# Attention times V over four query tiles at once instead of two, in a two-layer encoder

## The chip, the core and the metric

The kernel runs on one core of a Trainium2 chip, in one launch. The metric is the device time in microseconds, the median over several runs. The engines are called by the names that the profile uses: PE (matrix multiplication, with PEld for its weight loads), DVE (vector), ACT (scalar functions and copies), POOL (a second, slower vector engine) and SP, which here only issues transfers.

## The reference, cut to what matters

Two layers work on 1024 tokens of width 1024, one sequence, float32. Each normalizes, projects, runs a bidirectional attention with 8 heads, gates the result with SiLU(z), projects out and adds to the residual.

```python
# layer 0, differential attention, per block of 128 queries
sc = einsum('bqhcd,bkhcd->bhcqk', qb, k) * scale      # two score maps per head, c = 0, 1
p = softmax(sc, axis=-1)
p = p[:, :, 0] - lam * p[:, :, 1]
o = einsum('bhqk,bkhd->bqhd', p, v)                   # v: 1024 keys x 128 per head
# then RMSNorm of each head's 128 values, gate, output projection

# layer 1, latent attention (MLA)
sc = (einsum('bqhd,bkhd->bhqk', qn, k_nope) + einsum('bqhr,bkr->bhqk', qp, k_pe)) * scale
o = einsum('bhqk,bkhd->bqhd', softmax(sc, axis=-1), v)
```

The part in question is the last product of each layer, P times V ("PV" below).

## The kernel before, in words

**Precision.** A float32 product is made of three matmuls of a fast format: each operand is split in a high part and a low rest, and high x high, high x low and low x high are summed in PSUM (`mm3`). So everything that goes into a matmul exists twice (`pth` and `ptl` for P transposed, the two halves of `vt` for V).

**Tiles of an attention.** A head has 1024 queries: eight tiles of 128, in two halves of four. For each tile, scores against all 1024 keys are built in PSUM (eight matmuls of 512 columns in layer 0, where there are two score maps; ten in layer 1), DVE takes the negative row maximum (L393), ACT the exponential with its row sum (L395). In layer 0 DVE then combines both maps into `e` (L775), and the next tile's first maximum is queued behind that; the second map's PSUM buffer is held until then. PE turns `e` around by transposes, four blocks of 128 x 128 into one PSUM bank (L376, bank `tr`, a single buffer), ACT copies the bank into `pth` (L378) and DVE subtracts that into `ptl` (L379). A tile takes two such turns, `kh` = 0 for the first 512 keys and 1 for the rest.

**PV before.** V is the weight (a 128 x 128 block for each key tile, high or low), P^T the moving operand, and the result o^T stands in one PSUM bank per half (`pv`, 512 columns). Two query tiles share a set of four P^T buffers, each of four key tiles x 256 columns (4 KB per partition), out of six. So PV runs for every second tile, with 256 columns: 8 key tiles x 3 matmuls for a pair, in two parts of 12 (`kh` = 0 and 1). When both pairs of a half are done, `close` normalizes and gates the half.

**The order of work.** It is written out by hand in `after_scores` and `run_tails`. With tile i's scores, the tile before (`last`) gets its first turn behind the scores, the one before that (`prev`) its second turn amid the scores, and PV of `prev`, if it is the second of a pair, follows. Between these points stand numbers of filler steps from the tables `FILL0`, `FILL1` (six or four per tile, eight tiles per head) and `FILL7` (layer 0's last head): a step is three matmuls of 512 columns of the projection that feeds the next head (queries, keys, gate z), with the transfers of its weights, their splitting on ACT and POOL, and the copies of its result. In each layer's last head, steps of the output projection (`Pre.step`, six matmuls) are run from the seventh tile on. Behind the loop `run_tails` finishes the last two tiles. A scheduler with its own cost model then orders the instructions of each engine by the program's order and its estimate of when each is ready, so that an engine's order in the trace is not always that of the program.

**V.** Layer 1 has its values for heads 4 to 7 computed and stored to DRAM shortly before its attention starts (`v1_tile`, `store_v`), through temporary tiles that live in the P^T buffers' pool (tag "pt"). `load_v` brings a head's V back, two transfers of 512 KB, into three buffers.

The functions that the change touches:

## Time and profile before

| | before |
|---|---|
| device time, median of 3 runs | 1458.1 us (1456.93 to 1460.11) |
| profiled execution, span from first to last instruction (its only time) | 1457.5 us |
| PE busy | 1396.9 us, 96% |
| PE weight loads busy | 1166.4 us, 80% |
| DVE, ACT, POOL busy | 63%, 50%, 43% |
| matmuls | 7388, of which 1536 are PV |

Layer 0's attention with its filler lies at about 178 to 705 us of the span, layer 1's at about 1010 to 1368. In a row of instructions in order of time there stand the start in us, the duration in us, engine, line, operation, what it writes and reads, shape and count (x4: four merged in one row); in brackets the idle time of the engine just before and what ended it. In a row of groups there stand the count, the busy time in us, the mean duration of one in ns and the idle time before. A row of stretches gives for each engine the busy us and the number of instructions, then the granted clock of PE, the share of the transfer engines in use and GB/s. Matmuls overlap in the pipeline: the duration of one is longer than the distance to the next.

### The profile page before, as it was taken

The numbers are of one execution on the slowest core, as the hardware profiler recorded it, in microseconds if no ns is written. First come the engines' busy times: TensorE is split into PE (matmuls) and PEld (weight loads), VectorE is DVE, ScalarE is ACT, GpSimd is POOL, SyncE is SP. The second block draws the span as 40 slices with busy tenths as digits, with TensorE's granted clock in tenths as the row PEclk, the third lists the DMA queues.
The fourth block names the chain that finished last, engine by engine and source line by source line (L and its number), as shares of the span: only waits on it lengthen the run. The fifth ranks groups of instructions, "written<-read, shape, count | busy, mean of one in ns | idle before, by whom it ended". The sixth has DMA issues, their size and how long they took to land. (4 is left out here: it accounts for less than half of the span.)

```text
span 1457.5 us, 20649 instructions
## 1 busy us (share of the span) xinstructions
PE 1396.9 (96%) x7388; PEld 1166.4 (80%) x7388; DVE 917.9 (63%) x1362; ACT 727.8 (50%) x1287; POOL 627.6 (43%) x493
## 2 busy tenths in 40 slices
PE   5999999999999999998999879989999999999997
PEld 4778788888888887886787768867888888888886
DVE  6656777767777767687355964544666555555355
ACT  5622365656566665565343433334455554545342
POOL 4416164656465555543641455422141331412572
PEclk9999999999999999999999989999999999999999
DMA  9787723333332424237743145398443432336563
GB/s 329 228 252 237 245 67 99 85 99 87 102 93 82 114 68 117 59 87 261 253 144 123 44 152 173 107 289 211 146 125 123 118 104 65 110 97 215 181 234 141
DMA packets 135527, 213.70 MB, mean 147 GB/s; under 512 B 19072, under 2 KB 56064, under 8 KB 135424
## 3 DMA queue, kind: packets, MB, share of 16 engines
q1 hardware_dynamic: 135424, 212.38, 47.7%
q8 instruction: 58, 0.95, 0.3%
q14 instruction: 45, 0.37, 0.1%
HBM read 137.92 MB, written 50.80 MB: 129 GB/s over the span
## 5 line engine op out<-in xcount | busy, mean ns | idle before, releaser
L378 ACT CAST pth<-tr 128x512 fp32r<-128x512 f32 x256 | 150.3, 587 | 281.7 <-PE tr L376 280.0
L393 DVE TENSOR_REDUCE nm<-s 128x1 f32<-128x1024 f32 x192 | 234.0, 1219 | 76.8 <-PE s L767 65.7
L379 DVE TENSOR_TENSOR ptl<-tr,pth 128x512 fp32r<-128x512 f32 x256 | 176.1, 688 | 140.1 <-ACT pth L378 139.6
L224 POOL TENSOR_TENSOR wl<-wraw,wh 128x512 fp32r<-128x512 f32 (+2 forms) x81 | 106.8, 1321 | 210.7 <-ACT wh L223 202.2
L395 ACT ACTIVATE e<-s,nm 128x1024 f32<-128x1024 f32 x128 | 143.7, 1122 | 31.8 <-DVE nm L393 26.2
L376 PE MATMUL tr<-ident,e 128*128 128x128 f32 x1024 | 154.6, 273 | 2.2 <-DVE ptl L379 1.9
L376 PEld LDWEIGHTS tr<-ident,e 128*128 128x128 f32 x1024 | 121.5, 140 | 42.9 <-DVE ptl L379 19.4
L178 PE MATMUL acc<-h0h,wh 128*128 128x512 f32 x360 | 150.8, 419 | 3.6 <-DVE v_hl L356 3.1
L178 PE MATMUL pv<-pth,vt 128*128 128x256 f32 x512 | 147.2, 287 | 0.0
L179 PE MATMUL pv<-ptl,vt 128*128 128x256 f32 x512 | 145.6, 284 | 0.0
L180 PE MATMUL pv<-pth,vt 128*128 128x256 f32 x512 | 144.6, 282 | 0.0
L180 PE MATMUL acc<-h0h,wl 128*128 128x512 f32 x360 | 142.8, 397 | 0.3 <-POOL wl L224 0.3
L179 PE MATMUL acc<-h0l,wh 128*128 128x512 f32 x360 | 142.1, 395 | 0.0
L1007 POOL TENSOR_TENSOR wol<-wor,woh 128x512 fp32r<-128x512 f32 x64 | 85.6, 1360 | 83.3 <-ACT woh L1006 78.9
L179 PEld LDWEIGHTS pv<-ptl,vt 128*128 128x128 f32 x512 | 97.7, 191 | 2.6
L178 PEld LDWEIGHTS pv<-pth,vt 128*128 128x128 f32 x512 | 97.6, 191 | 2.8 <-ACT pth L378 0.2
L180 PEld LDWEIGHTS pv<-pth,vt 128*128 128x128 f32 x512 | 97.7, 191 | 0.1
L320 POOL TENSOR_TENSOR rp_r<-rp_raw,cosT 128x512 f32<-128x512 f32 x38 | 49.8, 1311 | 94.9 <-ACT rp_raw L315 51.7
L325 POOL TENSOR_TENSOR rp_sw<-rp_sw,sinT 128x512 f32<-128x512 f32 x42 | 55.7, 1326 | 77.8 <-DMA rp_sw<-rp_raw 73.0
L767 PE MATMUL s<-ks,qa 128*128 128x512 f32 x256 | 82.0, 402 | 3.0 <-DVE e L775 2.7
L775 DVE SCALAR_TENSOR_TENSOR e<-s,z,e 128x1024 f32<-128x1024 f32 x64 | 82.1, 1283 | 2.1
L767 PE MATMUL s<-ks,qb 128*128 128x512 f32 x256 | 80.9, 395 | 0.0
(590 smaller groups left out, 3365.2 us busy)
## 6 DMA issues: line engine op xcount, KB each, us to landing
ada<-in_ada_ss SPq DMA_DIRECT2D x32, 512.0 KB, 5.8
wraw<-in_w_s SPq DMA_DIRECT2D x64, 256.0 KB, 2.9
vS<-v_hl SPq DMA_DIRECT2D x32, 512.0 KB, 5.3
vt<-vS SPq DMA_DIRECT2D x32, 512.0 KB, 3.9
wor<-in_w_out SPq DMA_DIRECT2D x64, 256.0 KB, 4.0
rp_sw<-rp_raw SPq DMA_DIRECT2D x168, 64.0 KB, 2.0
bc_s<-bc_d SPq DMA_DIRECT2D x34, 256.0 KB, 4.4
oS<-bc_s SPq DMA_DIRECT2D x30, 256.0 KB, 3.0
```

What stands on the lines that cost most here:

```text
L178: PE.matmul(psum, ah, bh, start=first, stop=False)
L179: PE.matmul(psum, ah, bl, start=False, stop=False)
L180: PE.matmul(psum, al, bh, start=False, stop=last)
L224: sub = (V if pair_of else G).tensor_sub(l_[:, :n], raw[:, :n], f32v(h_[:, :n]))
L376: PE.transpose(tr[:, j, :], p[:, kt * P : (kt + 1) * P], ident)
L378: mk["S"] = S.copy(pth[kh][:, :, dst], tr).ins
L379: mk["V"] = V.tensor_sub(ptl[kh][:, :, dst], tr, f32v(pth[kh][:, :, dst])).ins
L393: mk["V"] = V.reduce_max(nm, s_ps, axis=AX.X, negate=True).ins
L395: mk["S"] = S.activation(e, s_ps, AF.Exp, bias=nm, scale=1.0, accum_out=zs).ins
L767: PE.matmul(s_ps[:, kc * HF : (kc + 1) * HF], src[:, c, ql], KS[h][kc][:, c, :], start=fst, stop=not fst)
L775: combined.append(V.scalar_tensor_tensor(out=e0, in0=e1, scalar=z1[:, 0:1], in1=e0, op0=ALU.mult, op1=ALU.add).ins)
L1007: in_turn(G.tensor_sub(lo, raw, f32v(hi)))
```

## The change

PV runs once for four query tiles, with 512 moving columns: 8 key tiles x 3 matmuls for a half. P^T has four buffers of four key tiles x 512 columns (8 KB per partition), which are one half's high and low parts for both `kh`; each `kh` pair is allocated at the first tile's turn. The first part of PV (`kh` = 0) stands behind the fourth tile's first turn and two filler points later, the second part in the tile after. Within a part the order is no longer three matmuls per key tile, but all four key tiles of high x high, then low V x high P, then high V x low P. The filler tables are rewritten with the same sums per head. The V1 temporaries are halves of the larger P^T tiles (`vbuf`). The scratch for transfer descriptors is set to 1024 bytes.

```diff
@@ -38,8 +38,9 @@
 DEF = 7
 ROT = 3
 DEF1 = 0
-FILL0 = ((1, 2, 1, 1, 1, 0), (1, 1, 1, 1, 1, 1)) * 3 + ((1, 2, 1, 1, 1, 0), (1, 1, 1, 1, 1, 0))
-FILL1 = ((1, 0, 1, 0), (0, 1, 0, 0)) * 4
+FILL0 = ((1, 1, 1, 1, 1, 0), (1, 1, 1, 1, 1, 0), (1, 2, 1, 2, 1, 0), (1, 2, 1, 1, 1, 1)) + (
+    (1, 1, 1, 1, 1, 0), (1, 1, 1, 1, 1, 0), (1, 2, 1, 2, 1, 0), (1, 2, 1, 1, 1, 0))
+FILL1 = ((0, 1, 1, 0), (0, 0, 0, 0), (1, 1, 0, 0), (1, 0, 1, 0)) * 2
 SPL1 = 2
 Z_PRE = 16
 V_LATE = 6
@@ -55,7 +56,7 @@
 OP1 = (12, 4)
 LAST = [(((0, 1, 2, 3), 0, HF),), (((0, 1), 0, HF), ((2,), 0, HF), ((3,), 0, 256), ((3,), 256, HF))]
 Z_LAST = 4
-FILL7 = ((0, 1, 1, 1, 1, 0),) * 4
+FILL7 = ((0, 0, 0, 1, 1, 0), (0, 0, 0, 1, 0, 0), (0, 0, 0, 1, 0, 0), (0, 0, 0, 1, 0, 0), (0, 0, 0, 1, 1, 0))
 G_WAIT = 3
 G1_AT = 7
 VB = (2, 3)
@@ -351,7 +352,7 @@
             SP.dma_start(f32v(t[0:64, 1, :]), f32v(t[64:128, 1, :]))
 
     def store_v(l, sp, acc, tt, fh, tag="vst", bufs=None):
-        v = sp.tile([P, 2, HF], F32R, name="v_hl", tag=tag, bufs=bufs or VB[l])
+        v = sp() if callable(sp) else sp.tile([P, 2, HF], F32R, name="v_hl", tag=tag, bufs=bufs or VB[l])
         S.copy(v[:, 0, :], acc)
         V.tensor_sub(v[:, 1, :], acc, f32v(v[:, 0, :]))
         th, tl = tt // 4, tt % 4
@@ -379,13 +380,12 @@
         mk["V"] = V.tensor_sub(ptl[kh][:, :, dst], tr, f32v(pth[kh][:, :, dst])).ins
 
     def pv(o_, vt, pth, ptl, kh):
-        for j in range(4):
-            mm3(o_, vt[kh][:, 0, j, :], vt[kh][:, 1, j, :], pth[kh][:, j, :], ptl[kh][:, j, :], kh + j == 0, kh * 4 + j == NT - 1)
+        for lhs, rhs in ((0, pth), (1, pth), (0, ptl)):
+            for j in range(4):
+                PE.matmul(o_, vt[kh][:, lhs, j, :], rhs[kh][:, j, :], start=kh == j == lhs == 0 and rhs is pth, stop=kh == 1 and j == 3 and rhs is ptl)
 
     def alloc_pt(ap_):
-        pth = [ap_.tile([P, 4, 2 * P], F32R, name="pth", tag="pt", bufs=6) for _ in range(2)]
-        ptl = [ap_.tile([P, 4, 2 * P], F32R, name="ptl", tag="pt", bufs=6) for _ in range(2)]
-        return pth, ptl
+        return [ap_.tile([P, 4, 4 * P], F32R, name=n, tag="pt", bufs=4) for n in ("pth", "ptl")]
 
     def softmax_part(ap_, s_ps, zs, bufs=3):
 
@@ -863,30 +863,30 @@
     class Tail:
 
 
-        def __init__(self, qp, t, e, zz, c):
-            self.qp, self.t, self.e, self.zz, self.c = qp, t, e, zz, c
-            self.mate = tails[1]
+        def __init__(self, half, t, e, zz, c):
+            self.half, self.t, self.e, self.zz, self.c = half, t, e, zz, c
 
         def turn(self, kh):
-            if kh == 0:
-                self.pt = alloc_pt(self.c["pool"]) if self.t == 0 else self.mate.pt
-                self.mate = None
-            transpose_p(self.e, *self.pt, self.t, kh)
+            c = self.c
+            if self.t == 0:
+                if kh == 0:
+                    c["pt", self.half] = [], []
+                for d_, t in zip(c["pt", self.half], alloc_pt(c["pool"])):
+                    d_.append(t)
+            transpose_p(self.e, *c["pt", self.half], self.t, kh)
 
         def pv(self, kh):
-            c, qp = self.c, self.qp
-            if self.t == 0:
+            c = self.c
+            if self.t < 3:
                 return
             if kh == 0:
-                if qp == 0:
+                if self.half == 0:
                     c["vt"] = load_v(c["pool"], c["l"], c["h"])
-                if qp % 2 == 0:
-                    c["o_"] = bank("pv", "pv")
-                    c["open"](qp // 2)
-            cs = slice((qp % 2) * 256, (qp % 2) * 256 + 256)
-            pv(c["o_"][:, cs], c["vt"], *self.pt, kh)
-            if kh == 1 and qp % 2 == 1:
-                c["close"](qp // 2, c["o_"], self.zz)
+                c["o_"] = bank("pv", "pv")
+                c["open"](self.half)
+            pv(c["o_"], c["vt"], *c["pt", self.half], kh)
+            if kh == 1:
+                c["close"](self.half, c["o_"], self.zz)
 
     tails, hooks = [None, None], []
 
@@ -896,12 +896,10 @@
         prev.turn(1)
         fill(0)
         last.turn(0)
-        prev.pv(0)
-        prev.pv(1)
         fill(1)
         last.turn(1)
+        last.pv(0)
         fill(2)
-        last.pv(0)
         last.pv(1)
         tails[:] = [None, None]
 
@@ -911,12 +909,12 @@
         if last:
             last.turn(0)
         fill(n)
-        if prev:
-            prev.pv(0)
-        fill(n + 1)
         new = hooks[:]
         if prev:
             prev.pv(1)
+        fill(n + 1)
+        if last:
+            last.pv(0)
         fill(n + 2)
         for f in new:
             hooks.remove(f)
@@ -959,7 +957,7 @@
                     fill(2)
                     after_scores(fill, 3)
                 side.tick()
-                tails[:] = [tails[1], Tail(qp, t, e0, zz, ctx_)]
+                tails[:] = [tails[1], Tail(half, (qp * 2 + t) % 4, e0, zz, ctx_)]
                 if extra:
                     extra(qp * 2 + t)
         if late:
@@ -1131,7 +1129,7 @@
         head_out(o_, o, sq)
         return lambda: subln(o, sq, zz, 1, NH - 1, OT[NH - 1][1])
 
-    tail0 = attn0(NH - 1, lambda i: FILL7[i] if i < Z_LAST else (0,) * 6, extra0, late0)
+    tail0 = attn0(NH - 1, lambda i: FILL7[i] if i <= Z_LAST else (0,) * 6, extra0, late0)
     mk.clear()
     load_ot(OT[NH - 1][0], [oS[0][NH - 1, 0, i] for i in range(2)])
     st2b.close()
@@ -1625,7 +1623,7 @@
                     e = scores1(h, half, ti, zz)
                     fill(0)
                     after_scores(fill, 1)
-                tails[:] = [tails[1], Tail(qp, t, e, zz, ctx_)]
+                tails[:] = [tails[1], Tail(half, ti, e, zz, ctx_)]
                 if extra:
                     extra(qp * 2 + t)
         if late:
@@ -1636,9 +1634,17 @@
 
     stream1.step(6)
     v1_left = list(range(NT))
+    vbufs = []
+
+    def vbuf():
+        if not vbufs:
+            t = ap.tile([P, 4, 4 * P], F32R, name="v_hl", tag="pt", bufs=4)
+            vbufs.extend([t[:, :2, :], t[:, 2:, :]])
+        return vbufs.pop(0)
+
     for n, steps in zip(V1_AT, (steps1[0] - 6, 0)):
         for tt in v1_left[:n]:
-            v1_tile(tt, 1, ap, "pt", 6)
+            v1_tile(tt, 1, vbuf)
         del v1_left[:n]
         stream1.step(steps)
     side.flush()
@@ -1646,7 +1652,7 @@
     zz0 = sm.tile([P, 4], F32, name="zz1")
     first1 += [zz0, scores1(0, 0, 0, zz0)]
     for tt in v1_left:
-        v1_tile(tt, 1, ap, "pt", 6)
+        v1_tile(tt, 1, vbuf)
     stv.close()
     ap2 = pool(st5, "attn1b")
     for h in range(NH - 1):
@@ -1805,7 +1811,7 @@
     import concourse.bacc as bacc
     from concourse.bass_utils import run_bass_kernel_spmd
 
-    nc = bacc.Bacc("TRN2", target_bir_lowering=False, num_devices=1)
+    nc = bacc.Bacc("TRN2", target_bir_lowering=False, num_devices=1, dynamic_dma_scratch_size=1024)
     A = layout(inputs)
     arrays, aps = {}, {}
     for name, a in A.items():
```

## The prediction

> **What bounds the kernel now.** I read the page's totals and slices first, then the busy time by stages, then TensorE's (PE's) own order of time, since a "busy" PE says nothing about its pace.
>
> ```profile
> span 1457.5 us, 20649 instructions
> PE 1396.9 (96%) x7388; PEld 1166.4 (80%) x7388; DVE 917.9 (63%) x1362; ACT 727.8 (50%) x1287; POOL 627.6 (43%) x493
> L178 PE MATMUL pv<-pth,vt 128*128 128x256 f32 x512 | 147.2, 287 | 0.0
> L179 PE MATMUL pv<-ptl,vt 128*128 128x256 f32 x512 | 145.6, 284 | 0.0
> L180 PE MATMUL pv<-pth,vt 128*128 128x256 f32 x512 | 144.6, 282 | 0.0
> ```
>
> ```profile
> core 0: us, PE busy (x) PEld busy (x) DVE busy (x) ACT busy (x) POOL busy (x), PEclk, DMA share, GB/s
> 178.00:560.00 382.00, 381.69 (x2150) 325.76 (x2150) 278.42 (x398) 236.86 (x418) 216.83 (x179) 1.00 0.33 90
> 560.00:650.00 90.00, 88.32 (x493) 74.06 (x491) 64.83 (x90) 55.33 (x97) 46.64 (x38) 1.00 0.33 91
> 650.00:705.00 55.00, 49.95 (x292) 41.42 (x291) 32.46 (x54) 29.71 (x54) 25.20 (x22) 1.00 0.67 234
> 1010.00:1110.00 100.00, 99.89 (x602) 85.05 (x601) 65.10 (x96) 53.27 (x97) 28.13 (x21) 1.00 0.52 147
> 1110.00:1320.00 210.00, 210.00 (x1278) 180.44 (x1277) 115.52 (x162) 107.76 (x197) 57.04 (x45) 1.00 0.36 103
> 1320.00:1368.00 48.00, 48.00 (x305) 41.75 (x304) 25.49 (x36) 25.47 (x46) 15.94 (x12) 1.00 0.51 163
> ```
>
> The two attentions lie in these windows. PE is without a gap in all of them but the second and third, at a granted clock of 1.00, and VectorE (DVE) is busy for 278 of 382 us at most. So in both attentions PE's own work sets the time, except in the last head of the first attention (650 to 705), where PE lacks 5 us. The profiled execution has a span of 1457.5 us and shows no other time of its own; the median of the runs is 1458.1, 0.6 above it. I sum against the span and add the 0.6.
>
> **PV, the main term.** There are 1536 matmuls of 256 columns (3 x 512), and the change makes of them 768 of 512 columns: half as many weight loads, the same number of columns. The group rows tempt one to take 284 ns for each; that is how long one takes from end to end, and they overlap. What counts is the distance between starts:
>
> ```profile
> 300.29 0.28 PE L178 MATMUL pv<-pth,vt 128*128 128x256 f32 x1
> ...
> 301.61 0.28 PE L180 MATMUL pv<-pth,vt 128*128 128x256 f32 x1
> 301.72 0.39 PE L178 MATMUL acc<-h0h,wh 128*128 128x512 f32 x1
> ...
> 303.85 0.39 PE L178 MATMUL acc<-h0h,wh 128*128 128x512 f32 x1
> ...
> 304.55 0.39 PE L767 MATMUL s<-ks,qa 128*128 128x512 f32 x1
> ...
> 694.38 0.39 PE L178 MATMUL oacc<-woh,oth 128*128 128x512 f32 x1
> ...
> 702.36 0.39 PE L180 MATMUL oacc<-woh,otl 128*128 128x512 f32 x1
> ```
>
> Twelve PV matmuls take 301.72 - 300.29 = 1.43 us, 119.2 ns each. Matmuls of 512 columns with a weight load each stand (304.55 - 303.85)/3 = 233 ns apart in the input projection and (702.36 - 694.38)/35 = 228 ns in the output projection. No row shows a PV of 512 columns; these two are its bounds, and I take the middle, 230.5. Two old ones then cost 238.4 and a new one 230.5: 7.9 ns saved, 768 times, is 6.1 us (4.1 to 8.0 between the bounds). Half a sequence (four query tiles) goes from 5.72 to 5.53 us, and there are 32 halves.
>
> [...]
>
> **The last head of the first attention.** There PE waits for a chain on DVE, and PV can hide in it:
>
> ```profile
> 651.49 1.28 DVE L775 SCALAR_TENSOR_TENSOR e<-s,z,e 128x1024 f32<-128x1024 f32 x1
> 658.01 1.28 DVE L775 SCALAR_TENSOR_TENSOR e<-s,z,e 128x1024 f32<-128x1024 f32 x1
> 664.80 1.28 DVE L775 SCALAR_TENSOR_TENSOR e<-s,z,e 128x1024 f32<-128x1024 f32 x1
> ```
>
> One query tile ends with each of these lines, 6.52 and 6.79 us apart whatever PE has to do: a floor of some 6.6 us a tile. PE's own work for a tile is eight score matmuls (1.85 us at 231 ns), two groups of four transposes (0.44 each: in the rows of layer 1 below 1319.19 to 1319.55, plus 0.08 by which the pair of matmuls behind is longer than the 0.46 of 1322.39 to 1322.85), so 2.72, plus 0.69 for a filler step of three matmuls, plus PV. Old, by tile index 0 to 7 (the four, then the last three of the seven left filler steps go to tiles 0 and 1; 24 PVs or 2.86 at tiles 1, 3, 5, 7; one output-projection step of 1.39 at 6 and 7): 6.6, 7.7, 6.6, 6.6, 6.6, 6.6, 6.6, 7.0, then 2.86 of PV behind the last transposes: 57.1 us. New (steps 2, 1, 1, 1, 2 at tiles 0 to 4; 12 PVs or 2.77 at tiles 0, 1, 4, 5): 6.9, 6.6, 6.6, 6.6, 6.9, 6.6, 6.6, 6.6, then a whole half, 5.53: 58.9 us. So +1.8 here. That the tail has PE time with nothing to hide it stands in these rows: PV follows the last transposes, and the output projection follows PV without a gap (694.38 above).
>
> ```profile
> 690.96 0.60 PE L376 MATMUL tr<-ident,e 128*128 128x128 f32 x4
> 691.32 0.36 PE L178 MATMUL pv<-pth,vt 128*128 128x256 f32 x1
> ```
>
> Before that head, where PE is full, 27 old PVs of 2.86 (77.2 us) become 13 halves of 5.53 (71.9): -5.3. First attention: -3.5. Second, full throughout: 16 x 0.19 = -3.0.
>
> **The new wait.** PV's first part for a half now starts on the P^T of the tile transposed just before it; the old one started on a pair transposed a tile earlier. The path is transposes, ACT's copy (L378), PV:
>
> ```profile
> 360.68 0.60 PE L376 MATMUL tr<-ident,e 128*128 128x128 f32 x4
> 361.32 0.59 ACT L378 CAST pth<-tr 128x512 fp32r<-128x512 f32 x1 [1.01 <-PE tr L376]
> ...
> 530.63 0.60 PE L376 MATMUL tr<-ident,e 128*128 128x128 f32 x4
> 532.99 0.58 ACT L378 CAST pth<-tr 128x512 fp32r<-128x512 f32 x1
> ...
> 564.80 0.60 PE L376 MATMUL tr<-ident,e 128*128 128x128 f32 x4
> 567.54 0.58 ACT L378 CAST pth<-tr 128x512 fp32r<-128x512 f32 x1
> ...
> 601.00 0.60 PE L376 MATMUL tr<-ident,e 128*128 128x128 f32 x4
> 603.35 0.58 ACT L378 CAST pth<-tr 128x512 fp32r<-128x512 f32 x1
> ```
>
> These are the fourth tiles of four halves. P^T is there 1.2 us after the group began in the first, 2.9 to 3.3 in the others, where ACT came to it late. Between transposes and PV stand two filler steps in both layers (2 x 0.69 + 0.44 = 1.8 us). So the usual copy is covered with 0.6 to spare and a late one misses by 1.1 to 1.5. DVE's lower half of P^T is read only by the last four of twelve matmuls, eight (1.85 us) later, and is covered too. Queued behind a waiting PV on PE are the next tile's scores, and for them wait DVE's maximum and ACT's exponential. But the order on PE is a planner's, which moves ready work into such holes; here it has put the first three score matmuls of the next tile ahead of transposes that had to wait:
>
> ```profile
> 1319.19 0.60 PE L376 MATMUL tr<-ident,e 128*128 128x128 f32 x4
> 1319.55 0.71 PE L1587 MATMUL s<-kps,qpa 128*128 128x512 f32 x2
> 1320.09 0.62 PE L1587 MATMUL s<-kps,qpb 128*128 128x512 f32 x2
> 1320.55 0.62 PE L1587 MATMUL s<-kn_h,qn_h 128*128 128x512 f32 x2
> 1321.01 0.40 PE L1587 MATMUL s<-kn_l,qn_h 128*128 128x512 f32 x1
> 1321.24 0.61 PE L376 MATMUL tr<-ident,e 128*128 128x128 f32 x4
> ...
> 1322.39 0.61 PE L1587 MATMUL s<-kps,qpa 128*128 128x512 f32 x2
> 1322.85 0.62 PE L1587 MATMUL s<-kps,qpb 128*128 128x512 f32 x2
> ```
>
> So the price is between -1.7 (always filled, and the idle of 560 to 650 gone with the old order) and 3 x 1.5 in the first attention plus 2 x 0.8 (1.2 less the 0.44 of the transposes) in the second's last head, which has no filler steps: 6.1 us. I take 1.0, near the lower end, because the nearest rows, those of that last head, show the hole filled.
>
> **Edits that cost nothing.** Four buffers hold one half exactly. The next half's first tile overwrites what PV's first part read one tile earlier and what the second part read most of a tile earlier: 1.85 us of scores at least lie between, as cover. The filler steps in heads 0 to 6 sum to 47 a head before and after (12 in the second attention) and fall behind by at most two (10 for 12); each carries its strip's share of weight loads on SP, of ACT casts and of POOL's subtractions. Two steps are 1.4 us; a strip is fetched 16 steps (11 us) ahead, so that is the cover. The V loads (two a head) are moved from the fourth tile's turn to the fifth's in program order, past other loads on SP; their buffers come free when the previous head's PV ends, at its successor's tiles 0 and 1, four tiles (over 26 us) before use. First four tiles of head 0 have no PV now but 5, 5, 7, 7 steps: for tiles 1 to 3, 19 steps x 0.69 + 7.8 = 20.9 us of PE work over a floor of 19.8, so no gap. The halves of the V1 stores take as much memory as before, eight tiles in eight slots. The smaller DMA scratch changes no instruction: every transfer in the page's list of issues is SP's.
>
> **The sum.** -3.5 - 3.0 + 1.0 = -5.5 us: 1457.5 becomes 1452.0, and 0.6 above that, 1452.6, is the median I expect; I write 1452.5. About 0.2% (2.9 us) is what a measurement of this kernel can tell from no change.
>
> **The rivals.**
> *A smaller gain, the same time.* If the new PV runs at the 233 ns of the input projection, it saves 4.1 instead of 6.1; if the waits cost 3 besides, the sum is -1.5: about 1456.5. For it: three of the late copies above are of just the tile that now matters. Against: the output projection's 228. 0.2, of which 0.03 for a fixed part per matmul of a few ns only, so that joining two saves little: at 236 ns a new PV the pair saves 2.4 and all of them 1.8 us, which with the same terms as in the sum is 1.2 less than before, 1457. [...]
>
> *Slower: PV waits for the copy.* One mechanism: ACT runs its exponential ahead of the copy at the fourth tile of every half of the first attention, and the planner, which believes its own times, puts nothing in front. 16 halves x 1.5 = 24 us, less 6.5 won: 1475. It decides from 6 halves on (6 x 1.5 = 9.0 against 6.5 + 2.9 to be seen as slower). For it: the three late copies. Against: all windows of the first attention before its last head lack 2.0 us of PE together (0.3 and 1.7), late copies and all. 0.11.
>
> *A larger gain.* Old tiles alternated between 2.72 + 6 x 0.69 = 6.9 us of PE work without PV, just above the floor of 6.6, and 9.7 with it; new ones have 7.6 and 8.9. If that ends the gaps of 560 to 650 (1.7 us) and the last head's even order saves half of its 5 us, the sum is -9.7: 1448.5. 0.15.
>
> *The 284 ns are real.* Then 437 us of PV would become some 305 (at the 395 ns or so that such a matmul of 512 columns takes from end to end, 0.39 in the rows at 694 to 702) and the time 1326. The starts above refute it: 0.
>
> **Chances.** Forecast (1450 to 1455) 0.54, larger gain 0.15, same 0.2, slower 0.11. Faster takes the first two, 0.69. The range leaves out the slower rival and the outer part of the larger gain: 1448 to 1458.5; the likeliest case alone spans 1450 to 1455.
>
> **What would show it.** Right: 768 PV matmuls of 512 columns at 228 to 233 ns between starts; windows of both attentions still at a full PE and some 3 us shorter each; the last head of the first attention no shorter. Wrong: idle time before PV in the groups' rows, released by ACT's L378, above 3 us in total; or starts above 236 ns, at which the main term halves.

## The result, and the profile after

The changed kernel takes 1466.0 us (median of 4 runs, 1464.29 to 1471.57) against 1458.3 for the kernel before on the same chip: ratio 1.0061 [1.004, 1.0082], 0.6% slower. Forecast were 1452.5. A copy of it, run again beside other kernels, gave 1468.05 and 1.0058 [1.0041, 1.0076].

The page of the kernel after: its span, the busy time of PE, and the two groups of PV (count, busy us, mean ns of one, idle before).

```profile
span 1469.8 us, 19084 instructions
PE 1398.1 (95%) x6620; PEld 1124.9 (77%) x6620; DVE 923.2 (63%) x1362; ACT 725.5 (49%) x1287; POOL 626.5 (43%) x493
L385 PE MATMUL pv<-pth,vt 128*128 128x512 f32 x512 | 137.5, 405 | 4.3 <-ACT pth L379 4.2
L385 PE MATMUL pv<-ptl,vt 128*128 128x512 f32 x256 | 69.6, 394 | 0.6 <-DVE ptl L380 0.6
```

(Line numbers have moved by one: L378 is now L379, L376 L377, L224 L225.) There are 768 matmuls fewer, as planned, but PE is busy no less, and PV now has idle time before it where it had none. The profiled execution (1471.57 us) is the longest of the four, so what follows explains its span, 12.3 us over that of before; in which stretch the shorter executions save their 5 us no trace shows.

Starts of the landmarks, in order of time, kernel before and then after: first scores of layer 0, last combine of its last head, first `rb` matmul behind that head, first scores of layer 1, last PV.

```profile
154.77 0.62 PE L767 MATMUL s<-ks,qa 128*128 128x512 f32 x2
...
686.90 1.28 DVE L775 SCALAR_TENSOR_TENSOR e<-s,z,e 128x1024 f32<-128x1024 f32 x1
...
705.96 1.13 PE L824 MATMUL rb<-sq,ones 128*128 128x128 f32 x8 [0.94 <-DVE sq L823]
...
994.96 0.73 PE L1587 MATMUL s<-kn_h,qn_h 128*128 128x512 f32 x2 [1.87 <-DVE qn_l L1539]
...
1365.92 0.28 PE L180 MATMUL pv<-pth,vt 128*128 128x256 f32 x1
```

```profile
155.97 0.62 PE L767 MATMUL s<-ks,qa 128*128 128x512 f32 x2
...
690.02 1.28 DVE L775 SCALAR_TENSOR_TENSOR e<-s,z,e 128x1024 f32<-128x1024 f32 x1
...
710.84 1.16 PE L824 MATMUL rb<-sq,ones 128*128 128x128 f32 x8 [0.85 <-DVE sq L823]
...
1001.18 0.73 PE L1585 MATMUL s<-kn_h,qn_h 128*128 128x512 f32 x2 [1.86 <-DVE qn_l L1537]
...
1375.83 1.07 PE L385 MATMUL pv<-ptl,vt 128*128 128x512 f32 x4
```

The attentions are measured here from their first scores, somewhat earlier than the windows of the prediction begin. The first attention goes from 551.2 to 554.9 us (first to third row), the second from 371.0 to 375.3 (fourth to last; the last of the x4 starts at 1376.5). Forecast were 548.7 and 368.0. The three stretches outside are 1.2, 1.3 and 1.7 us longer in this execution; in `q_behind` below, which has the same PV, the last two are 289.3 and 91.8 us, as before (289.0 and 91.6), so they do not belong to the change.

PE's waits (total us, times, longest), after, in 150 to 712 and then in 990 to 1380 us; and before, the same two stretches:

```profile
PE pv L385 <- ACT pth L379: 3.0, 4, 1.9
PE s L767 <- DMA qb<-qb: 1.8, 1, 1.8
PE s L767 <- issue: 1.6, 1, 1.6
...
PE acc L181 <- POOL wl L225: 2.1, 2, 1.7
PE s L1585 <- DVE qn_l L1537: 1.9, 1, 1.9
PE pv L385 <- ACT pth L379: 1.2, 2, 0.8
...
```

```profile
PE s L767 <- DVE e L775: 2.7, 3, 0.9
PE acc L178 <- DVE v_hl L356: 2.1, 1, 2.1
...
PE s L1587 <- DVE qn_l L1539: 1.9, 1, 1.9
```

All rows of the two lists add up to 13.5 and 6.3 us after, 9.5 and 1.9 before: 8.4 us more, at single places. Of them 5.1 are three waits where a head ends and the next one's queries or weights are wanted: 1.8 for `qb`, 1.7 for `wl`, and 1.6 before the first scores of the second head (222.17), to which the profile names no releaser; that head's queries were sent off at 217.78 to 220.52. Taken from the starts of all matmuls against their usual distances (231, 119.5 and 109 ns for 512, 256 and 128 columns), which counts small waits too, it is some 5.0 us more in the first attention and 6.6 in the second. Half clock, a granted clock of 0.50, adds 2.5 (5.7 us after, 3.2 before). 11.6 + 2.5 - 6.1 won by PV is 8.0, and that is by how much the two attentions grew. The clock shows in three rows of time and one of stretches (start and end, us, then busy us of PE, PEld, DVE, ACT, POOL, granted clock, share of the transfer engines, GB/s):

```profile
602.58 0.40 PE L181 MATMUL acc<-h0h,wl 128*128 128x512 f32 x1
604.92 3.63 PE L385 MATMUL pv<-pth,vt 128*128 128x512 f32 x8 [1.94 <-ACT pth L379]
608.34 0.49 PE L179 MATMUL acc<-h0h,wh 128*128 128x512 f32 x1
...
604.90:608.30 3.40, 3.38 (x8) 2.66 (x9) 3.01 (x3) 0.81 (x2) 2.70 (x3) 0.53 0.51 142
```

Behind a wait of 1.94 us the granted clock is 0.53 from 604.90 to 608.30: eight matmuls take 3.42 us, 427 ns each instead of 230, another 1.6 us. The same stands at 677 (0.50 from 676.80 to 680.20) and, for 6.8 us, at 1100 (0.51 from 1100 to 1107; 14 matmuls from 1101.37 to 1107.14: 5.77 us instead of 3.2). Before, the clock was full in both attentions but for the first 15 us of each.

### The profile page after: what moved, and what is told of

It reads as the page before. It is cut to its first block, busy times and chain, and to the rows that moved or that the text cites. A ratio compares the mean times of both kernels' runs of the same rounds, so it can differ in the third digit from the quotient of the medians.

```text
span 1469.8 us, 19084 instructions
## 1 busy us (share of the span) xinstructions
PE 1398.1 (95%) x6620; PEld 1124.9 (77%) x6620; DVE 923.2 (63%) x1362; ACT 725.5 (49%) x1287; POOL 626.5 (43%) x493
## 5 line engine op out<-in xcount | busy, mean ns | idle before, releaser
L379 ACT CAST pth<-tr 128x512 fp32r<-128x512 f32 x256 | 150.2, 587 | 283.0 <-PE tr L377 282.0
L225 POOL TENSOR_TENSOR wl<-wraw,wh 128x512 fp32r<-128x512 f32 (+2 forms) x81 | 105.8, 1309 | 228.9 <-ACT wh L224 212.9
L377 PE MATMUL tr<-ident,e 128*128 128x128 f32 x1024 | 155.6, 274 | 2.6 <-DVE ptl L380 2.5
L377 PEld LDWEIGHTS tr<-ident,e 128*128 128x128 f32 x1024 | 122.4, 141 | 45.1 <-DVE ptl L380 21.0
L385 PE MATMUL pv<-pth,vt 128*128 128x512 f32 x512 | 137.5, 405 | 4.3 <-ACT pth L379 4.2
L385 PEld LDWEIGHTS pv<-pth,vt 128*128 128x128 f32 x512 | 93.5, 192 | 31.1 <-ACT pth L379 13.8
L179 PEld LDWEIGHTS acc<-h0h,wh 128*128 128x128 f32 x360 | 68.0, 189 | 16.5 <-DVE v_hl L357 3.4
L181 PEld LDWEIGHTS acc<-h0h,wl 128*128 128x128 f32 x360 | 67.6, 188 | 16.2 <-POOL wl L225 1.1
L180 PEld LDWEIGHTS acc<-h0l,wh 128*128 128x128 f32 x360 | 68.1, 189 | 10.9
L805 POOL TENSOR_TENSOR o<-o,bc_s 128x512 f32<-128x512 f32 x30 | 47.3, 1575 | 62.2 <-DVE o L1603 54.8
```

Source lines behind the costliest of these rows:

```text
L179: PE.matmul(psum, ah, bh, start=first, stop=False)
L180: PE.matmul(psum, ah, bl, start=False, stop=False)
L181: PE.matmul(psum, al, bh, start=False, stop=last)
L225: sub = (V if pair_of else G).tensor_sub(l_[:, :n], raw[:, :n], f32v(h_[:, :n]))
L377: PE.transpose(tr[:, j, :], p[:, kt * P : (kt + 1) * P], ident)
L379: mk["S"] = S.copy(pth[kh][:, :, dst], tr).ins
```

## The experiments

Beside each kernel ran the kernel before; "first" and "second" are the lengths of the two attentions between the landmarks. To compare: before 551.2 and 371.0, after 554.9 and 375.3, the copy of after 557.0 and 375.8. Each is one profiled execution, and those of after and its copy, the same program, differ by 2.1 and 0.5 us; a difference of that size between two profiles says nothing.

**The change again** (`after_again`), no edit.

> The changed kernel once more, for a second trace of it. Its profiled execution lost 13.6 us to half clock inside the two attentions (three stretches behind waits of 1 to 2 us), where before had none; its other executions were 5 to 7 us shorter at a higher mean clock. If the half clock is an accident on top of steady new waits, this run shows waits at the same places, few or no half-clock stretches inside the attentions, and about 1464 to 1466 us. If the slow-down is the half clock alone, a run without it is at 1458 or below.

1.0058: the loss is there again, of the same size. The waits stand at the same places, and half clock came again, in four stretches of 3.4 us (from 678.5, 695.5, 1002.7 and 1105.1), so it was no accident of one execution. The 13.6 us of the expectation are the length of the stretches in the first trace; what they cost is the 5.7 us above.

**Is the width worth anything?** `narrow_pv` makes each PV matmul two of 256 columns and keeps all else of the change:

```diff
-                PE.matmul(o_, vt[kh][:, lhs, j, :], rhs[kh][:, j, :], ...)
+                for a in (0, 256):
+                    PE.matmul(o_[:, a : a + 256], vt[kh][:, lhs, j, :], rhs[kh][:, j, a : a + 256], ...)
```

> The changed kernel with each PV matmul of 512 columns done as two of 256 with the same weights, one after the other; all else as changed (four query tiles at once, four buffers, fillers). It measures the width by itself. If the width saves what the distances between starts say (2 x 119 against 230 ns, 768 times), this is 5 to 7 us slower than the changed kernel: 1471 to 1473. If the second attention's new waits hide that time, less, down to no difference: 1466.

1482.9, ratio 1.0163 [1.0136, 1.019]; first 561.6, second 382.0. So in this order of work the width gains some 15 us by the medians (the copy has 1468.05) and 8.9 by the two profiles (spans 1479.3 and 1470.4), in both cases more than the 6.1 of the distances alone. PV's waits for ACT's copy are among the rest: 5.2 us in the first attention, the longest 3.9, where the change has 3.0 and 1.9. The loss is not in the width.

**The tables of filler steps, alone and the other way round.** `old_fills` is the change with the old FILL0 and FILL1, `fills_on_before` the kernel before with the new ones (the other direction of the same lines).

```diff
 old_fills:
-FILL1 = ((0, 1, 1, 0), (0, 0, 0, 0), (1, 1, 0, 0), (1, 0, 1, 0)) * 2
+FILL1 = ((1, 0, 1, 0), (0, 1, 0, 0)) * 4
...
```

> The changed kernel with the filler tables of before in heads 0 to 6 of both layers; the last head of layer 0 keeps its new table. Theory A (the moved filler steps bring the next head's Q, K and weight pieces later, and PE waits for these): the waits for the Q transfer and for POOL's weight halves go, and the time falls to about 1458 or below. Theory B (PV waits for the copy of the P^T transposed just before): no help in layer 0, where the two steps between stand in the old table too, and worse in layer 1, where one of two is gone: 1466 to 1472.

> The kernel before (PV for two tiles, 256 columns, six buffers of 4 KB) with the changed filler tables of heads 0 to 6 of both layers. Theory A (the moved fillers cost by themselves): 1465 or more. If fillers only have to fit the rhythm of PV: some loss too, since the new table gives the tile with PV five steps and not the one without, 1461 to 1465; if they cost nothing, 1458 to 1461.

`old_fills` 1475.35, 1.01 [1.0079, 1.0121]: the new tables suit the new PV better than the old ones. `fills_on_before` 1468.09, 1.005 [1.0033, 1.0068]: on the old PV the new tables alone cost 8 us, all in the second attention (551.0 and 378.2), with a 3.5 us wait of PE for POOL's `wl`. Tables and PV are tied to each other; moved filler steps are not free in either kernel. `old_fills` has a wait of 3.6 us for `wl` at the same place (1097.7), so the new tables and the new PV each bring that wait alone.

**The wait of PV for the copy.** `pv_later` moves PV's first part into the next tile; `fixed_rhs` gives PV a constant tile as moving operand, so that PV waits for no P^T (PV's content is left out); `pt5` has five P^T buffers; `j_major` has the old order of the products.

```diff
 pv_later:   prev, last = tails
+        if prev:
+            prev.pv(0)
...
-        if last:
-            last.pv(0)
 fixed_rhs:
-                PE.matmul(o_, vt[kh][:, lhs, j, :], rhs[kh][:, j, :], ...)
+                PE.matmul(o_, vt[kh][:, lhs, j, :], FIX[l][:, j, :], ...)
 pt5:
-        ... tag="pt", bufs=4) for n in ("pth", "ptl")]
+        ... tag="pt", bufs=5) for n in ("pth", "ptl")]
 j_major:
-        for lhs, rhs in ((0, pth), (1, pth), (0, ptl)):
-            for j in range(4):
+        for j in range(4):
+            for lhs, rhs in ((0, pth), (0, ptl), (1, pth)):
```

> The changed kernel with PV's first part of each half moved from behind the fourth tile's first turn to the next tile, in front of that tile's first turn; four buffers still. The copy that PV reads is then a tile old. Theory B (that new wait, and the half clock that follows it): the waits of PV on ACT's copy go (4.8 us in the profiled execution of the changed kernel, with 10 us of half clock behind two of them): 1458 or below. Theory A (moved fillers): PV's waits go but the time stays within 2 us of the changed kernel, 1464 to 1467. Cost against it: the next half's first turn has to wait until PV's first part has read its buffers.

> The changed kernel with PV's moving operand taken from a constant tile (the cosine table, written once per layer) instead of P^T; all transposes, copies and subtractions of P^T still run, so only PV's two dependencies on P^T are gone (PV waits for no copy, and no copy waits for PV). What it computes for PV is left out. Theory B' (the loss is made by these dependencies, directly or through the order that a planner builds around them): 1452 to 1456, below before. Theory C (it is made elsewhere: fillers, the order of ACT's, DVE's and POOL's queues, weights): 1463 to 1468, as the changed kernel.

> The changed kernel with five P^T buffers of 8 KB instead of four. Theory D (four buffers are one half exactly, and the next half's first turns are held up by PV's reading): falls by 3 us or more, to 1464 or below. If buffers bind nowhere: within 2 us of the changed kernel's 1468 of this chip.

> The changed kernel with PV's matmuls in the old order, key tile by key tile with their three products, so that the low part of P^T is needed by the second matmul of a part and not by the ninth. If PV's reading of fresh P^T is what costs (B'), worse than the changed kernel by 0.7 us (DVE's subtraction) at each half that waits: 1470 to 1480. If not, within 2 us of it.

1470.03 (1.0062 [1.004, 1.0083]), 1468.18 (1.0052 [1.0036, 1.0067]), 1469.2 (1.0066 [1.0043, 1.0088]) and 1479.49 (1.0131 [1.0108, 1.0155]). PE's waits in `fixed_rhs`, first attention and then second:

```profile
PE tr L377 <- DVE ptl L380: 3.2, 3, 1.6
PE rb L832 <- DVE sq L831: 3.0, 1, 3.0
...
PE acc L181 <- POOL wl L225: 3.2, 2, 2.8
```

With the wait of PV gone, other waits stand near the same places (1.6 us of the transposes at 606.4, 2.8 for `wl` at 1101.1): PE came to PV earlier and then stood at the next thing that was late. The two attentions are 553.7 and 373.2 us in this profile, 3.3 and 2.6 less than in the copy, but the stretch between them is 3.4 longer (291.9, with half clock from 709.0, at the `rb` wait), and the time is the same. In `pv_later` PV's waits in the first attention fall to 0.7 us, and the scores wait 4.7 us for DVE's combine instead. So the 4.2 us before PV are where the lateness shows, not where it comes from. Where the longest of them, 1.94 us at 604.92, comes from stands in the rows of DVE and ACT, kernel after:

```profile
599.23 2.02 DVE L330 TENSOR_TENSOR rp_r<-rp_r,rp_sw 128x512 f32<-128x512 f32 x1 [0.67 <-POOL rp_sw L326]
...
601.28 0.62 ACT L338 CAST ks<-rp_r 64x512 fp32r<-64x512 f32 x1 [1.77 <-DVE rp_r L330]
...
603.18 1.09 ACT L395 ACTIVATE s<-s,nm 128x1024 f32<-128x1024 f32 x1
...
604.29 0.57 ACT L379 CAST pth<-tr 128x512 fp32r<-128x512 f32 x1
```

The first row ends the rotation of the next head's keys (the four transfers, two POOL products and the DVE addition that turn each projected half of queries or keys). It waits for POOL's product, ACT's cast of its result waits 1.77 us for it, and behind that cast stand a second one, a copy, an exponential and only then the copy that PV needs, 4.9 us behind its transposes (599.38). Before, the same casts stood ahead of the same copy, but the addition and the first cast had no wait, and the copy came 2.35 us behind its transposes (601.00, 603.35). In the copy of after, in `pt5` and in `q_behind` below, the cast waits 2.2 to 2.3 us and PV 2.4; in `narrow_pv` it is 3.6 and 3.9. So this wait hangs on the rotation.

A fifth buffer changes nothing in the time: the four were enough. `j_major`, whose second matmul of a part needs DVE's lower half already, is 11 us slower than the change: the new order of products earns its place.

**Is the next head's Q too late?** In the change the first scores of the last head of layer 0 wait for `qb`. Rows of POOL, SP and PE, after:

```profile
628.71 1.29 POOL L348 TENSOR_TENSOR qb<-rp_r,qa 64x512 fp32r<-64x512 f32 x1
...
631.64 0.55 SPq L352 DMA_DIRECT2D qb<-qb  x1
635.41 0.70 PE L767 MATMUL s<-ks,qb 128*128 128x512 f32 x2 [1.77 <-DMA qb<-qb]
```

Before, the same subtractions stood 4.4 us earlier in the span, and the scores started without a wait:

```profile
624.28 1.30 POOL L347 TENSOR_TENSOR qb<-rp_r,qa 64x512 fp32r<-64x512 f32 x1
...
630.67 0.62 PE L767 MATMUL s<-ks,qb 128*128 128x512 f32 x2
```

Counted to the moment at which PE had come to these scores (633.64 after, 630.67 before), the first subtraction starts 4.9 us ahead after and 6.4 before. So the queries are 1.5 us later, and the rest of the 4.4 is that all of the kernel runs later by then.

`DEF` says by how many filler steps the last part of a finished projection (the addition, the casts and subtractions, the transfers out) is put off. `def5` has 5 instead of 7, `before_def9` is the kernel before with 9; all steps keep their number. `fill1_front` moves layer 1's steps to earlier tiles of a head, `front_def5` does both.

```diff
-DEF = 7
+DEF = 5
-FILL1 = ((0, 1, 1, 0), (0, 0, 0, 0), (1, 1, 0, 0), (1, 0, 1, 0)) * 2
+FILL1 = ((0, 1, 1, 0), (1, 0, 0, 0), (1, 1, 1, 0), (1, 0, 1, 0), (0, 1, 1, 0), (1, 0, 0, 0), (1, 0, 0, 0), (0, 0, 0, 0))
```

> The changed kernel with Q and K of the next head in the first attention finished 5 instead of 7 steps after their projection. Theory E: the waits of a head's first scores for Q's transfer (1.8 us at the last head, 1.6 at the second) go, the first attention falls by 3 to 4 us, the time to about 1464. Theory F: no gain, 1466 to 1470, since POOL's and DVE's queues then take Q's work ahead of other work that is due.

> The kernel before with Q and K of the next head in the first attention finished 9 instead of 7 steps after their projection, nothing else: about 2 us later, as much as the shorter end of a head costs in the changed kernel. Theory E: the same waits for Q's transfer appear at the heads' first scores, and the kernel is slower by 2 to 4 us, 1462 to 1464. If Q has slack there: unchanged, 1460.

> The changed kernel with the second attention's filler steps moved to the front of each head (2, 1, 3, 2, 2, 1, 1, 0 steps for the eight tiles instead of 2, 0, 2, 2, 2, 0, 2, 2). Theory E (the last tiles of a head have become short, since PV now runs in its tiles 0, 1, 4, 5, so the next head's Q, made by the steps of tiles 5 and 6, comes 6 us later beside the first scores than before, and the next weight piece is queued on POOL behind Q's subtractions): the wait for POOL's weight half at about 1097 goes with the half clock behind it, the second attention falls from 375.5 to 368 to 371 us, the time to 1461 to 1464. Theory F (any other order makes its own accidents): a wait of the same size elsewhere, 1466 to 1470.

> Both of the above together. Theory E: the gains add, to 1457 to 1461. Theory F: 1466 to 1470.

1478.15 (1.0132 [1.0105, 1.0158]), 1459.82 (1.0014 [1.0003, 1.0026]), 1470.1 (1.0087 [1.0062, 1.0112]) and 1478.06 (1.0135 [1.0116, 1.0155]). In `def5` the wait for `qb` is gone, and the first attention is 562.5 us all the same: its scores now wait 7.8 us for DVE's combine, 5.1 of them at 648.6. DVE ahead of that, in `def5`:

```profile
644.88 1.99 DVE L330 TENSOR_TENSOR rp_r<-rp_r,rp_sw 128x512 f32<-128x512 f32 x1 [4.36 <-POOL rp_sw L326]
...
647.28 1.28 DVE L775 SCALAR_TENSOR_TENSOR e<-s,z,e 128x1024 f32<-128x1024 f32 x1
```

The combine is queued behind the rotation's addition, and that waits for POOL. Over the first attention DVE waits 31.3 us for such products in `def5` (21 times), 5.7 in the change (8 times) and 2.8 before (4 times). `before_def9` gets a wait of 1.9 us for `qa` and a first attention no longer than before (549.4). `fill1_front` does not do what it was made for: PE waits 2.6 us for `wl` at 1096.5, and the second attention is 376.2 us. So the one late transfer is not the owner of the loss either, and pulling its chain forward pushes DVE's other work back.

**The chains beside PE, left out in both kernels.** Here the comparison is pair against pair. `before_norope` and `after_norope` leave out the rotation of queries and keys; `before_nomax` and `after_nomax` leave out the row maximum (a constant bias instead, scale 0.001). In the expectations E is the theory of POOL's queue in layer 1, F that of the planner's order as a whole, G that of DVE's maximum.

```diff
 norope:
-        for q in range(4):
-            SP.dma_start(sw[q * 32 : q * 32 + 32], raw[(q ^ 1) * 32 : (q ^ 1) * 32 + 32])
-        r_ = eng.tensor_mul(r, raw, cosT[:, cs])
...
-            in_turn(G.tensor_mul(sw, sw, sinT[:, cs]))
...
-                V.tensor_add(r, r, sw)
-            return r
+            return raw
 nomax:
-        mk["V"] = V.reduce_max(nm, s_ps, axis=AX.X, negate=True).ins
-        mk["S"] = S.activation(e, s_ps, AF.Exp, bias=nm, scale=1.0, accum_out=zs).ins
+        mk["S"] = S.activation(e, s_ps, AF.Exp, bias=zero, scale=0.001, accum_out=zs).ins
```

> The kernel before with the rotation of Q and K left out everywhere (its four transfers, two POOL products and one DVE sum per projected half; the plain projection is used). The base of a pair. No theory tells its own time; less side work, so 1445 to 1458.

> The changed kernel with the same left out. Theory E (the next head's Q chain, with POOL's queue, comes too late for the shortened end of a head): it is now faster than its pair by 4 to 7 us, as the distances between PV's matmuls say. Theory F (every change of PE's work makes a new order on all engines, and its waits are scattered): slower than its pair by 3 to 10 us, as with the rotation.

> The kernel before without the softmax's row maximum (192 DVE instructions of 1.22 us; the exponential takes a constant bias and a scale of 0.001, to stay finite). The base of a second pair; the last head of the first attention loses its floor of 6.6 us a tile, so about 5 us less than before and more if PE waits elsewhere on that chain: 1448 to 1455.

> The changed kernel with the same left out. Theory G (the waits come from ACT's queue, where exponentials that wait for DVE's maximum hold back the copies of P^T that PE needs; in the first attention ACT's exponentials wait 25 us for the maximum in the changed kernel against 16 before, in the second 11 against 3): faster than its pair by 4 to 7 us. Theory F: slower than its pair by 3 to 10 us.

Without rotation: 1455.47 (0.9971 [0.9955, 0.9987]) and 1455.08 (0.9965 [0.9953, 0.9977]): the two are equal, where with rotation the change costs 8 us. E had forecast a gain of 4 to 7 us and F a loss of 3 to 10; neither came. Without maximum: 1469.34 (1.0065 [1.0046, 1.0083]) and 1480.4 (1.0139 [1.0123, 1.0155]): the change costs 11 us there, so G falls, and leaving out some other work does not by itself take the loss away. PE's waits in the second attention, `after_norope` (its partner has none):

```profile
PE acc L181 <- POOL wl L225: 1.8, 1, 1.8
PE pv L375 <- ACT pth L369: 0.4, 1, 0.4
PE tr L367 <- DVE ptl L370: 0.4, 1, 0.4
```

The second attention is 370.5 us against 368.9 of its partner, and the first 555.1 against 556.0; at its start a wait for V's rest takes 5.7 us after and 3.9 before, and without those the change wins 2.7 there, of 3.5 forecast. In the second, 3.0 less was forecast and 1.6 more came; the wait for POOL's `wl` is 1.8 of these 4.6 us.

**POOL's queue at the end of a head of layer 1.** POOL in order of time, before:

```profile
1088.21 1.75 POOL L347 TENSOR_TENSOR qpb<-rp_r,qpa 64x512 fp32r<-64x512 f32 x1
1090.03 1.28 POOL L348 TENSOR_TENSOR qpb<-rp_r,qpa 64x512 fp32r<-64x512 f32 x1
1091.39 0.73 POOL L224 TENSOR_TENSOR wl<-wraw,wh 128x256 fp32r<-128x256 f32 x1
```

After, with the PE row that waits for the last of them:

```profile
1097.32 1.26 POOL L348 TENSOR_TENSOR qpb<-rp_r,qpa 64x512 fp32r<-64x512 f32 x1 [1.28 <-ACT qpa L346]
1098.66 1.27 POOL L349 TENSOR_TENSOR qpb<-rp_r,qpa 64x512 fp32r<-64x512 f32 x1
1100.01 0.72 POOL L225 TENSOR_TENSOR wl<-wraw,wh 128x256 fp32r<-128x256 f32 x1
...
1100.78 0.79 PE L181 MATMUL acc<-ckh,wl 128*128 128x512 f32 x1 [1.74 <-POOL wl L225]
```

The head's first scores start at 1091.88, and the subtractions of its queries' rest stand 5.4 us behind that (0.9 before it in the old kernel, whose scores start at 1089.1). The weights of the next filler step are queued behind them, PE waits, and at 1100.05, within that wait, half clock sets in. `fills_on_before` has the same order on POOL (subtractions at 1097.81 and 1099.15, `wl` at 1100.48). `q_behind` puts the remaining filler steps of a head ahead of that late work of its queries; `norope_q_behind` is the same without rotation.

```diff
+        stream1.step(sum(steps1[: h + 2]) - stream1.count)
         while late_q:
             late_q.pop(0)()
-        stream1.step(sum(steps1[: h + 2]) - stream1.count)
```

> The changed kernel with two lines at the end of a head of the second attention exchanged: the remaining filler steps are issued before the next head's rotated Q is finished, not behind it, so that on POOL the weight piece that PE needs next stands in front of Q's two subtractions of 1.3 us. Theory E for the second attention (POOL's queue there makes the largest single wait, 2.0 us at about 1098, with half clock behind it): this wait goes, the second attention falls from 375.5 to 370 to 372 us, the time from about 1467 to 1462 or 1463. Theory F: a wait of its size elsewhere, 1466 to 1470.

> The changed kernel with the rotation of Q and K left out and the same two lines exchanged. Its pair is the kernel before without the rotation (1455.5). Theory E in full (the side work of the fillers, the rotation chain and POOL's queue, eats what the wider PV saves): with both out of the way 1449 to 1452, faster than its pair by 4 to 6 us as the distances between the matmuls say. Theory F: 1455 or more.

POOL and PE in `q_behind`:

```profile
1096.65 1.17 POOL L225 TENSOR_TENSOR wl<-wraw,wh 128x256 fp32r<-128x256 f32 x1
1097.97 1.30 POOL L348 TENSOR_TENSOR qpb<-rp_r,qpa 64x512 fp32r<-64x512 f32 x1
...
1097.87 0.50 PE L181 MATMUL acc<-ckh,wl 128*128 128x512 f32 x1 [1.31 <-POOL wl L225]
```

`wl` is now ahead of the subtractions, PE waits for it 1.31 us instead of 1.74, no half clock follows, and the second attention is 371.5 us, 3.8 less than in the change. Not all of that is the queue's. `pt5` has POOL's old order and the old wait:

```profile
1097.86 0.72 POOL L225 TENSOR_TENSOR wl<-wraw,wh 128x256 fp32r<-128x256 f32 x1
...
1098.64 0.50 PE L181 MATMUL acc<-ckh,wl 128*128 128x512 f32 x1 [1.75 <-POOL wl L225]
```

But its granted clock stays at 1.00 there, and its second attention is 372.4 us. So some 1 us of the 3.8 belongs to the order of the queue, and the rest to half clock, which stands at such a wait in the change (1.74 us) and does not in `pt5` (1.75). E holds for layer 1 in kind: POOL's queue makes this wait. The time is 1465.79, 1.0043 [1.0027, 1.0059], above the 1462 to 1463 that E expected; the interval overlaps that of the change, so the time alone does not show a gain. `norope_q_behind`: 1454.12 (0.9956 [0.9941, 0.9971]), above the 1449 to 1452 expected; its profile (of its shortest execution; span 1449.7, partner 1454.0) has 552.7 us for the first attention with a start wait of 4.0, which, the start waits apart, is 3.4 less than the partner (3.5 forecast; some 0.9 of it is half clock at the start, 3.4 us long here and 6.8 in the partner), and 369.2 for the second, where 3.0 less was forecast and 0.3 more came. Counted by starts as above, that second attention loses 3.4 us more than its partner's, in pieces of which PE's list of waits has only 0.9; what makes them no run here shows.

No kernel here that computes everything beats the one before.

## Why the prediction was wrong

**The main term held.** Four PV of 512 columns in a row, kernel after, and what follows them:

```profile
1036.88 1.08 PE L385 MATMUL pv<-ptl,vt 128*128 128x512 f32 x4
1037.80 0.60 PE L377 MATMUL tr<-ident,e 128*128 128x128 f32 x4
```

(1037.80 - 1036.88)/4 = 230 ns, and 230 is the median of 684 such distances too; forecast 230.5. No run shows the fixed part of only a few ns per matmul with which one rival came to 236 ns; the rows have 230.

**The last head of layer 0 held in direction, not by its working.** The forecast of +1.8 was -0.9 in its eight tiles and +2.7 behind them (5.53 for 2.86). From the last combine of the head before to its own last one it is 58.1 us before and 56.9 after, -1.2; from there to the first `rb` 19.1 and 20.8, +1.8 (22.4 in the copy). Together that is +0.6 (+2.5 in the copy), with a stretch of half clock in it. The floor of 6.6 us a tile, on which the working stands, was none: from 641.21 on, combines of the changed kernel follow one another in 6.45, 6.32, 6.17 and 6.00 us.

**The new wait was under-priced, and it is not the cause.** Forecast 1.0 us; PE's waits for `pth` are 4.2, with the half clock behind the longest 5.8 (4.2 + 1.6). That is above the 3 us set as the sign of a wrong forecast. But the rival that named this wait priced 16 halves at 1.5 us each, and it came at six places, and `fixed_rhs`, which takes it away, gains nothing. That rival did not happen either. The longest of these waits comes from the rotation, as the rows at 599 to 604 show.

**The step that failed is "Edits that cost nothing".** It put the new filler tables and the moved PV at nothing; with everything computed the change costs 8 us where 5.5 were to be won. It took the filler steps for PE work whose only deadline is the fetch of a strip of weights, 11 us ahead. It looked at what a step needs, and not at what comes out of it: the product of a step goes through ACT, four transfers, two products and two subtractions on POOL and more transfers before the next head's scores can use it, and POOL's queue holds the weights of later steps behind that. PV now lies in the first two tiles of each half, so that the tiles that end a head are short, and the next head begins before its queries are ready. With the rotation out of both kernels the 8 us are gone, within what the intervals tell; that is shown. Within it, `wl` behind the late subtractions accounts in layer 1 for some 1 us by itself (`q_behind` against `pt5`) and for some 4 where half clock comes with it (`q_behind` against the change).

**The clock was left out.** The prediction had no price for half clock: there were three stretches of it, 1.6 + 1.6 us lost in the first attention and 2.5 in the second, where the kernel before lost 1.6 at the start of each.

**What stays open.** `q_behind`, the best variant that does all of the work, is still 6 us over the kernel before. Most of that lies in the first attention (556.5 against 551.2), which no edit of the change, with the rotation in, brought below 553.7. That the rotation's chain makes the waits there late is shown by leaving the whole of it out, and for the wait at 604.92 by the rows of DVE and ACT; which of its links (POOL, the transfers, ACT's order) would have to move for the time to fall was not tried. The forecast gain of 5.5 us came in no run: without the rotation the two kernels are equal, and the 3.0 us of the second attention stay away even in `norope_q_behind`. The smaller DMA scratch was not tried alone; `after_norope` has it and is no slower than its partner. F, that the planner's order reacts as a whole, fits `before_nomax`, which has 192 DVE instructions less and is 0.65% slower, but it was not tested by an order of its own.

## What to carry to other kernels

Cost a moved filler step by when its product is due downstream, through every queue on the way, and not by the fetch of its inputs alone; and ask what is queued behind that work on the side engines. Work that moves between tiles also moves the deadlines: tiles that get shorter at the end of a head pull the next head's operands forward. A gain of 0.4% on PE is no larger than what such a reordering cost here (8 us, 0.5%, for the new tables alone on the old PV); leaving the suspected side chain out of both kernels, and comparing pair with pair, says quickly whether it is the owner.

## What the hardware showed that was not expected

Half clock stands at some of PE's waits of 1 to 2 us, and not at others as long. In the kernel after, it begins at 605.12, 0.2 us behind a wait of 1.94 us; at 676.80, 2.0 us behind one of 0.95 (ending at 674.83); and at 1100.05, within one of 1.74 (ending at 1100.78) that has another of 0.76 two us before it. It lasts 3.4, 3.4 and 6.8 us. Waits of 1.60 (222.17) and 1.77 (635.41) had none behind them, and in `pt5` neither did one of 2.41 us (603.87) at the place of the first. The wait of 1.94 us and the 1.6 us lost to half clock behind it are 3.5 us together.

The stretches are of a few lengths only. The three starts above stand 71.68 and 423.25 us apart, 21 and 124 times 3.413 us. In the traces of before and after the granted clock is 0.50 for 3.413, 6.827 or 10.240 us at a time, and the stretches at 1.00 between are whole multiples of 3.413 us; only the stretch that the end of the span cuts off is not. Why the clock fell at some waits and not at others, no run here shows.

Less work took longer here: without its 192 row maxima the kernel before needs 0.65% more. Its second attention grew from 371.0 to 377.7 us, with a wait that was not there before at the head of its list:

```profile
PE pv L180 <- DMA vt<-vS: 2.2, 1, 2.2
```
